# FFN heads: low parts of seven weight chunks formed by an adding DMA, and the last tile's norm and stores rearranged

## The chip, the core and the metric

The kernel runs on one core of a Trainium2 chip. The time is that of one execution on the device, in microseconds (us). The core's engines run side by side, each its own list of instructions: TensorE (PE, matrix products; PEld is its loading of weights), VectorE (DVE), ScalarE (ACT), GpSimd (POOL) and SyncE (SP, which here issues DMA transfers). They wait for each other through semaphores.

## The reference

Two layers on 512 tokens of width 1024, all in float32. Each layer has a mixer (layer 0: dilated attention beside a state-space model; layer 1: a recurrent block) and a SwiGLU feed-forward network (FFN) with 2816 hidden columns. Only the FFN and the norms around it matter here:

```
def rms_norm(x, g):
    y = x32 * lax.rsqrt(jnp.mean(x32 * x32, axis=-1, keepdims=True) + NORM_EPS) * g

def swiglu(x, w_gate, w_up, w_down):
    return (jax.nn.silu(x @ w_gate) * (x @ w_up)) @ w_down

for layer in range(DEPTH):
    ...
    hn = rms_norm(x, norm_ffn_pre[layer])
    ff = swiglu(hn, ffn_w_gate[layer], ffn_w_up[layer], ffn_w_down[layer])
    x = x + rms_norm(ff, norm_ffn_post[layer])
```

## The kernel before, in words

**Products in parts.** Every float32 operand of a matmul is split into a high part, rounded to the format `fp32r` that PE reads, and a low part, the raw value minus the high part. A product is then three matmuls: high by high, high by low, low by high. For weights the class `Chunk` does it, in half-chunks of 128x512 (four row blocks of 128 weights by 128 columns, 256 KB): the raw half is loaded by SP (L216), ACT copies it to the high part (L240), DVE subtracts the high part from the raw one (L241). Tiles are named after it: `wraw_`, `whi_`, `wlo_`, then the chunk.

**The FFN's entry** (`ffn_up`, called for layer 0 as `f0` and for layer 1 as `f1`). The weights of gate and up are taken as 44 column chunks of 128, gate and up in turn. The first four chunks (NFIRST) are multiplied half by half while the mixer's norm is still finishing the second half of the tokens; their banks carry the names `mo0b` and `mo1b`. Then come two "plain" chunks, `p4` (gate) and `p5` (up), 24 matmuls of 128x512 each into banks `f0b` (`f1b` in layer 1). Between these PE puts the norm's row, `bc_f`: four small matmuls that spread the reciprocal root `rsy_f` over the partitions. That root is made by DVE (`rst_f`, L380) from PE's sums `ns_mo` and raised to -1/2 by POOL (L383).

**The pairs.** The other 38 chunks are taken as pairs, one gate and one up chunk (n = 3 to 21), in a form of Strassen's scheme: seven products of half size instead of eight. `pair_weights` forms sums of the quarters of both chunks on DVE (L664 to L667) and makes four chunks of them: `a` (the gate chunk itself, but for a half that is used before and changed after), `c`, `d` (up) and `b`. On the side of the tokens ACT scales the inputs (`xa_f`, `xb_f`, L686 and L687), DVE forms the sums (L691 to L694), and ACT and DVE split them (`th_f`, `tl_f`). Products go to banks `f00b` to `f03b`. After the first products of a pair ACT copies out `pu_f` (L738) and `pv_f` (L742); only then may PE add the next products to the same banks ("onto").

**The end** (`ffn_last`). The down projection of layer 1 leaves each tile of 128 tokens in two banks of 512 columns. Per half, ACT sums squares (L850), POOL scales them (L852 for the first half, L854 and L855 for the second) and takes the power -1/2 (L856), DVE multiplies by the norm's weights (L858) and then by the root, adding the residual (L861); SP stores each half (256 KB).

**What sets the order.** The framework's scheduler orders each engine's list by its own estimates, except for stretches that the kernel pins to program order; the FFN's entry is not pinned. Weight tiles live in a pool of places that are handed on in the order in which they are given back; a load waits until the place's last reader is done. POOL has 58 instructions in the whole program and issues the small vector loads at the start on its own DMA queue; all weights come through SP's.

Of the kernel before, what the change touches and what calls it, by code (L numbers as in the profile page):

```python
# [19 lines left out]
P = 128  # L20
S = 512
# [73 lines left out]
def hybrid_trunk(  # L95
# [125 lines left out]
    class Chunk:  # L221


        def __init__(self, raw, nm, alloc=None, view=None, base=None, eng=None):
# [3 lines left out]
            for i, src in enumerate(raw.parts):  # L228
# [10 lines left out]
                if view is None:  # L239
                    act.activation(hi, src, AF.Copy)  # L240
                    eng.tensor_tensor(lo, src, hi.bitcast(F32), op=ALU.subtract)  # L241
# [376 lines left out]
    def ffn_up(layer, xh, xl, first, nsum, nm, hp):  # L618
# [37 lines left out]
        def pair_weights(n, alloc=None, base=None):  # L656

            r0, r1 = [Raw(NF, P, f"{nm}{n}{i}", cols2[2 * n + i][0][:, n * P:(n + 1) * P].rearrange(
                "(k p) n -> p k n", p=P), base=base) for i in range(2)]
            (a11, a12), (a21, a22) = r0.parts, r1.parts  # L660
            rs = Raw(NF, P, f"s_{nm}{n}", base=base)
# [11 lines left out]
        plain = [Chunk(Raw(NF, P, f"{nm}p{i}", cols2[i][0][:, cols2[i][1]:cols2[i][1] + P].rearrange(
            "(k p) n -> p k n", p=P), base=sb), f"{nm}p{i}",
            alloc=lambda name: hp.tile([P, S], F32R, tag=f"hh{next(own)}", name=name))
            for i in range(NFIRST, 2 * NPLAIN)]
# [26 lines left out]
        wa, wc, wd, wb = pair_weights(NPLAIN)  # L703
# [99 lines left out]
    def ffn_last(xh, xl, first, nsum):  # L803
# [37 lines left out]
        for t in range(NT):  # L841
# [4 lines left out]
            for h in range(2):  # L846
# [4 lines left out]
                if h == 0:  # L851
                    pool.tensor_scalar(s0, ss[:, 0:1], 1.0 / D, eps[:, t:t + 1], op0=ALU.mult, op1=ALU.add)  # L852
                else:
                    pool.tensor_scalar(r, ss[:, 1:2], 1.0 / D, None, op0=ALU.mult)  # L854
                    pool.tensor_tensor(r, r, s0, op=ALU.add)  # L855
# [4 lines left out]
            for h, y in enumerate(ys):  # L860
                dve.scalar_tensor_tensor(y, y, r, xk[2 * t + h], op0=ALU.mult, op1=ALU.add)  # L861
                nc.sync.dma_start(out[0, t * P:(t + 1) * P, h * 512:(h + 1) * 512], y)
# [838 lines left out]
```

## Time and profile before

| | |
|---|---|
| median of three timed runs | 1160.72 us (1160.39 to 1165.26) |
| profiled execution | 1165.47 us, span of its trace 1163.7 us |
| PE busy | 1117.9 us, 96% of the span |
| DVE busy | 887.0 us, 76% |
| ACT busy | 624.7 us, 54% |
| POOL busy | 25.1 us, 2% |
| 256 KB weight load on SP's queue, issue to landing | 2.7 to 4.8 us, median by tensor |

A row of the trace reads: start in us, duration in us, engine, line and operation, output<-inputs, partitions x elements, and in square brackets how long the engine had been idle ahead of it and which instruction ended that wait. "x4" after a row stands for four in a run of the same form. Matmuls overlap: the next one starts before the end of the one before is noted, so their rate is read from starts. An engine of 96% can still stand still at single places, and it is by stages that one sees where.

### The profile page before, as it was taken

The numbers are of one execution on the slowest core, as the hardware profiler recorded it, in microseconds if no ns is written. First come the engines' busy times: TensorE is split into PE (matmuls) and PEld (weight loads), VectorE is DVE, ScalarE is ACT, GpSimd is POOL, SyncE is SP. The second block draws the span as 40 slices with busy tenths as digits, with TensorE's granted clock in tenths as the row PEclk, the third lists the DMA queues.
The fourth block names the chain that finished last, engine by engine and source line by source line (L and its number), as shares of the span: only waits on it lengthen the run. The fifth ranks groups of instructions, "written<-read, shape, count | busy, mean of one in ns | idle before, by whom it ended". The sixth has DMA issues, their size and how long they took to land.

```text
span 1163.7 us, 19752 instructions
## 1 busy us (share of the span) xinstructions
PE 1117.9 (96%) x7310; PEld 992.1 (85%) x7310; DVE 887.0 (76%) x1899; ACT 624.7 (54%) x1280; POOL 25.1 (2%) x58
## 2 busy tenths in 40 slices
PE   6999899999899999999999999899999999999997
PEld 6877666889899999988889887689899999988886
DVE  7989675479999989882348877858999989884224
ACT  7556577357755554652344479644855455582221
POOL 1000010000000000000000000000000000000001
PEclk9999989999999999999999999899999999999999
DMA  8534410531433332433330432250243323324211
GB/s 212 144 118 134 107 47 1 162 92 28 125 105 94 96 101 83 122 98 97 118 100 10 118 96 85 65 171 19 79 122 94 107 76 107 119 92 127 91 64 72
DMA packets 165560, 113.42 MB, mean 97 GB/s; under 512 B 26852, under 2 KB 142296, under 8 KB 165464
## 3 DMA queue, kind: packets, MB, share of 16 engines
q1 hardware_dynamic: 162168, 109.95, 32.3%
q10 hardware_dynamic: 3040, 2.17, 0.7%
q8 instruction: 57, 0.93, 0.3%
q14 instruction: 39, 0.32, 0.1%
q0 software_dynamic: 256, 0.06, 0.0%
HBM read 103.75 MB, written 4.19 MB: 93 GB/s over the span
## 4 chain that ended last, share of the span: by engine, by line
PE 76%; ACT 8%; DVE 7%; DMA 6%; issue 2%; SPq 0%; ACTq 0%; DVEq 0%; POOLq 0%; POOL 0%
PE fo L170 10%; PE op_fd L170 10%; PE op_mo L170 7%; PE f12b L170 4%; PE f10b L170 4%; PE f02b L170 4%; PE f11b L170 4%; PE f00b L170 4%; PE f01b L170 4%; PE qkv L170 3%; DMA wraw_f<-in_ffn_w_gate_dram 2%; PE f03b L170 2%; PE f13b L170 2%; PE xbb L170 2%; PE ub L170 1%
## 5 line engine op out<-in xcount | busy, mean ns | idle before, releaser
L241 DVE TENSOR_TENSOR wlo_fo<-wraw_fo,whi_fo 128x512 fp32r<-128x512 f32 x44 | 30.2, 691 | 63.5 <-PE fo L170 60.6
L170 PE MATMUL op_fd<-hi_f,wlo_fd 128*128 128x512 f32 (+1 forms) x200 | 73.5, 367 | 0.0
L170 PE MATMUL op_fd<-lo_f,whi_fd 128*128 128x512 f32 (+1 forms) x200 | 73.4, 367 | 0.0
L170 PE MATMUL op_fd<-hi_f,whi_fd 128*128 128x512 f32 (+1 forms) x200 | 72.5, 369 | 0.0
L170 PE MATMUL fo<-wlo_fo,hi_f 128*128 128x512 f32 x176 | 69.5, 395 | 0.0
L170 PE MATMUL fo<-whi_fo,hi_f 128*128 128x512 f32 x176 | 69.3, 397 | 0.2 <-ACT whi_fo L240 0.2
L241 DVE TENSOR_TENSOR wlo_fd<-wraw_fd,whi_fd 128x512 fp32r<-128x512 f32 x44 | 30.1, 690 | 51.5 <-ACT whi_fd L240 45.1
L170 PE MATMUL fo<-whi_fo,lo_f 128*128 128x512 f32 x176 | 69.3, 394 | 0.0
L240 ACT ACTIVATE whi_fo<-wraw_fo 128x512 fp32r<-128x512 f32 x44 | 27.4, 631 | 71.7 <-DMA wraw_fo<-in_ffn_w_down_dram 46.6
L240 ACT ACTIVATE whi_fd<-wraw_fd 128x512 fp32r<-128x512 f32 x44 | 27.6, 628 | 60.4 <-DMA wraw_fd<-in_ffn_w_down_dram 36.5
L170 PEld LDWEIGHTS op_fd<-hi_f,whi_fd 128*128 128x128 f32 x200 | 37.6, 188 | 6.9 <-ACT hi_f L769 0.2
L170 PEld LDWEIGHTS op_fd<-hi_f,wlo_fd 128*128 128x128 f32 x200 | 37.6, 188 | 6.7
L170 PEld LDWEIGHTS op_fd<-lo_f,whi_fd 128*128 128x128 f32 x200 | 37.6, 188 | 6.7
L170 PE MATMUL qkv<-whi_qkv,xh_m 128*128 128x512 f32 x96 | 40.5, 427 | 0.0
L170 PEld LDWEIGHTS fo<-whi_fo,hi_f 128*128 128x128 f32 x176 | 33.1, 188 | 8.3 <-ACT whi_fo L240 0.6
L170 PEld LDWEIGHTS fo<-whi_fo,lo_f 128*128 128x128 f32 x176 | 33.1, 188 | 7.9
L170 PEld LDWEIGHTS fo<-wlo_fo,hi_f 128*128 128x128 f32 x176 | 33.0, 188 | 7.5
L170 PE MATMUL qkv<-wlo_qkv,xh_m 128*128 128x512 f32 x96 | 38.4, 400 | 0.0
L170 PE MATMUL qkv<-whi_qkv,xl_m 128*128 128x512 f32 x96 | 38.1, 397 | 0.0
L241 DVE TENSOR_TENSOR wlo_mo<-wraw_mo,whi_mo 128x512 fp32r<-128x512 f32 x32 | 21.4, 688 | 21.4 <-ACT whi_mo L240 21.4
L664 DVE TENSOR_TENSOR wraw_s_f<-wraw_f,wraw_f 128x512 f32<-128x512 f32 x38 | 26.0, 685 | 13.2 <-DMA wraw_f<-in_ffn_w_up_dram 11.3
L170 PE MATMUL op_mo<-y1l,whi_mo 128*128 128x256 f32 (+1 forms) x88 | 30.8, 349 | 4.1 <-DVE y1l L1628 4.1
(1922 smaller groups left out, 4197.2 us busy)
## 6 DMA issues: line engine op xcount, KB each, us to landing
wraw_f<-in_ffn_w_gate_dram SPq DMA_DIRECT2D x84, 256.0 KB, 3.1
wraw_f<-in_ffn_w_up_dram SPq DMA_DIRECT2D x84, 256.0 KB, 3.3
wraw_fd<-in_ffn_w_down_dram SPq DMA_DIRECT2D x44, 256.0 KB, 2.7
wraw_fo<-in_ffn_w_down_dram SPq DMA_DIRECT2D x44, 256.0 KB, 2.9
wraw_qkv<-in_ev_w_in_dram SPq DMA_DIRECT2D x24, 256.0 KB, 3.6
wraw_mo<-in_ev_w_out_dram SPq DMA_DIRECT2D x16, 256.0 KB, 4.8
wraw_xb<-in_od_w_in_dram SPq DMA_DIRECT2D x16, 256.0 KB, 2.8
wraw_gg<-in_od_w_in_dram SPq DMA_DIRECT2D x16, 256.0 KB, 3.0
```

The source lines that it names most:

```text
L170: self.pin(nc.tensor.matmul(o, lhsT=lhsT, rhs=rhs, start=start, stop=stop, **kw))
L240: act.activation(hi, src, AF.Copy)
L241: eng.tensor_tensor(lo, src, hi.bitcast(F32), op=ALU.subtract)
L664: dve.tensor_tensor(s1, a21, a22, op=ALU.add)
```

## The change: what it does

Seven half-chunks in each layer's FFN get their low part another way: both halves of `p4` and of `p5`, both halves of chunk `a` and the second half of chunk `d` of the first pair (n = 3). DVE's subtraction is gone. Instead ACT writes the negated raw half, rounded to `fp32r`, into the low part's tile, and POOL issues a DMA that loads the same half of the weights from memory once more and adds it to what lies there, so that raw minus high remains. These are the half-chunks whose raw values stand in memory as they are; the other chunks of the pair are sums made on the chip.

At the end, the two scalings of the sum of squares move from POOL to DVE, for every tile, and become two instructions instead of three; the power stays on POOL. For the last tile the final add and the store go in halves of 256 columns: four adds and four stores of 128 KB, and the second store of each pair is issued by ACT instead of SP.

```diff
@@ class Chunk
-        def __init__(self, raw, nm, alloc=None, view=None, base=None, eng=None):
+        def __init__(self, raw, nm, alloc=None, view=None, base=None, eng=None, dram=None):
...
                     act.activation(hi, src, AF.Copy)
-                    eng.tensor_tensor(lo, src, hi.bitcast(F32), op=ALU.subtract)
+                    if dram is not None and dram[i] is not None:
+
+                        act.activation(lo, src, AF.Copy, scale=-1.0)
+                        pool.dma_start(lo, dram[i], accum_op=ALU.add)
+                    else:
+                        eng.tensor_tensor(lo, src, hi.bitcast(F32), op=ALU.subtract)
...
+        def src_of(i):
+            w, c0 = cols2[i]
+            return w[:, c0:c0 + P].rearrange("(k p) n -> p k n", p=P)
+
+        def pair_weights(n, by_load=False):
...
-            return [Chunk(t, f"{nm}{n}{q}", alloc=alloc) for t, q in ((r0, "a"), (rs, "c"), (r1, "d"), (rt, "b"))]
+            same = {}
+            if by_load:
+                u, v = src_of(2 * n), src_of(2 * n + 1)
+                same = {"a": [u[:, 0:HK], u[:, HK:NF]], "d": [None, v[:, HK:NF]]}
+            return [Chunk(t, f"{nm}{n}{q}", dram=same.get(q))
+                    for t, q in ((r0, "a"), (rs, "c"), (r1, "d"), (rt, "b"))]
...
+        plain = [Chunk(Raw(NF, P, f"{nm}p{i}", src_of(i), base=sb), f"{nm}p{i}",
+                       alloc=lambda name: hp.tile([P, S], F32R, tag=f"hh{next(own)}", name=name),
+                       dram=[src_of(i)[:, 0:HK], src_of(i)[:, HK:NF]])
+                 for i in range(NFIRST, 2 * NPLAIN)]
...
-        wa, wc, wd, wb = pair_weights(NPLAIN)
+        wa, wc, wd, wb = pair_weights(NPLAIN, True)
@@ ffn_last
                 if h == 0:
-                    pool.tensor_scalar(s0, ss[:, 0:1], 1.0 / D, eps[:, t:t + 1], op0=ALU.mult, op1=ALU.add)
+                    dve.scalar_tensor_tensor(s0, ss[:, 0:1], 1.0 / D, eps[:, t:t + 1], op0=ALU.mult, op1=ALU.add)
                 else:
-                    pool.tensor_scalar(r, ss[:, 1:2], 1.0 / D, None, op0=ALU.mult)
-                    pool.tensor_tensor(r, r, s0, op=ALU.add)
+                    dve.scalar_tensor_tensor(r, ss[:, 1:2], 1.0 / D, s0, op0=ALU.mult, op1=ALU.add)
                     pool.tensor_tensor(r, r, neghalf[:, 0:1], op=ALU.pow)
...
             for h, y in enumerate(ys):
-                dve.scalar_tensor_tensor(y, y, r, xk[2 * t + h], op0=ALU.mult, op1=ALU.add)
-                nc.sync.dma_start(out[0, t * P:(t + 1) * P, h * 512:(h + 1) * 512], y)
+                for q in (HS if t == NT - 1 else [slice(0, S)]):
+                    dve.scalar_tensor_tensor(y[:, q], y[:, q], r, xk[2 * t + h][:, q], op0=ALU.mult, op1=ALU.add)
+                    c = h * 512 + q.start
+                    (nc.scalar if q.start else nc.sync).dma_start(
+                        out[0, t * P:(t + 1) * P, c:c + q.stop - q.start], y[:, q])
```

The scheduler rearranges the FFN's entry on all engines. Three places matter. In the rows below the numbers behind a name tell instances apart: `f0p4_0` is layer 0, chunk p4, first half. The layer 1 order is of the same kind.

On ACT, layer 0, from the first high part of a plain chunk on, before:

```order
L240 ACTIVATE whi_f0p4_0_3483<-wraw_f0p4_0_3479 128x512
L240 ACTIVATE whi_f0p4_1_3487<-wraw_f0p4_4_3481 128x512
L240 ACTIVATE whi_f0p5_0_3495<-wraw_f0p5_0_3491 128x512
L240 ACTIVATE whi_f0p5_1_3499<-wraw_f0p5_4_3493 128x512
L686 ACTIVATE xa_f00_3505<-xT_0_147,cols_143 128x512
L687 ACTIVATE xb_f00_3506<-xT_4_151,cols_143 128x512
```

and with the change:

```order
L240 ACTIVATE whi_f0p4_0_3483<-wraw_f0p4_0_3479 128x512
L243 ACTIVATE wlo_f0p4_0_3484<-wraw_f0p4_0_3479 128x512
L240 ACTIVATE whi_f0p4_1_3488<-wraw_f0p4_4_3481 128x512
L243 ACTIVATE wlo_f0p4_1_3489<-wraw_f0p4_4_3481 128x512
L240 ACTIVATE whi_f0p5_0_3497<-wraw_f0p5_0_3493 128x512
L243 ACTIVATE wlo_f0p5_0_3498<-wraw_f0p5_0_3493 128x512
L240 ACTIVATE whi_f0p5_1_3502<-wraw_f0p5_4_3495 128x512
L243 ACTIVATE wlo_f0p5_1_3503<-wraw_f0p5_4_3495 128x512
L699 ACTIVATE xa_f00_3509<-xT_0_147,cols_143 128x512
```

Four negations (L243) have come in between; `xa_f` (L686, now L699) stands four places later.

On PE, layer 0, the start of the plain chunks, before:

```order
L170 MATMUL f0b5_3654<-xh_mo00_2988,whi_f0p5_0_3495 128x512
L170 MATMUL f0b5_3654<-xl_mo00_2996,whi_f0p5_0_3495 128x512
L170 MATMUL f0b5_3654<-xh_mo00_2988,wlo_f0p5_0_3496 128x512
L170 MATMUL f0b5_3654<-xh_mo01_2989,whi_f0p5_0_3495 128x512
L170 MATMUL f0b5_3654<-xl_mo01_2997,whi_f0p5_0_3495 128x512
L170 MATMUL f0b5_3654<-xh_mo01_2989,wlo_f0p5_0_3496 128x512
```

and with the change:

```order
L170 MATMUL f0b4_3633<-xh_mo00_2988,whi_f0p4_0_3483 128x512
L170 MATMUL f0b4_3633<-xl_mo00_2996,whi_f0p4_0_3483 128x512
L170 MATMUL f0b5_3661<-xh_mo00_2988,whi_f0p5_0_3497 128x512
L170 MATMUL f0b5_3661<-xl_mo00_2996,whi_f0p5_0_3497 128x512
L170 MATMUL bc_f0_3472<-cst_63,rsy_f0_3468 128x128 x4
L170 MATMUL f0b4_3633<-xh_mo00_2988,wlo_f0p4_0_3484 128x512
L170 MATMUL f0b4_3633<-xh_mo01_2989,whi_f0p4_0_3483 128x512
```

Before, PE began with p5 and had its low part in third place; the `bc_f` group came after 25 matmuls. Now both chunks begin with their two products on the high part, the four `bc_f` come next, and the first product with a low part, that of p4's first half, is behind them.

On POOL, between the mixer's last root and the FFN's, with the change (before, `rsy_f0` followed `rsy_mo01` at once, and `rsy_fd00` came next):

```order
L388 TENSOR_TENSOR rsy_mo01_3222<-rst_mo01_3221,neghalf_133 128x2
L244 DMA wlo_f03a_1_3594<-in_ffn_w_gate_dram 128x4x128
L244 DMA wlo_f0p4_0_3484<-in_ffn_w_gate_dram 128x4x128
L388 TENSOR_TENSOR rsy_f0_3468<-rst_f0_3467,neghalf_133 128x4
L244 DMA wlo_f0p4_1_3489<-in_ffn_w_gate_dram 128x4x128
L244 DMA wlo_f0p5_0_3498<-in_ffn_w_up_dram 128x4x128
L244 DMA wlo_f0p5_1_3503<-in_ffn_w_up_dram 128x4x128
L244 DMA wlo_f03d_1_3611<-in_ffn_w_up_dram 128x4x128
L244 DMA wlo_f03a_0_3589<-in_ffn_w_gate_dram 128x4x128
L388 TENSOR_TENSOR rsy_fd00_7491<-rst_fd00_7490,neghalf_133 128x2
```

Two adding DMAs (L244) stand ahead of the root `rsy_f0` and five behind it, in the order in which POOL issues them. In layer 1 the order is the same.

More of the change, by code (lines that the diff above doesn't have):

```diff
@@ L654, in ffn_up @@
         mid()
-        def pair_weights(n, alloc=None, base=None):
-            r0, r1 = [Raw(NF, P, f"{nm}{n}{i}", cols2[2 * n + i][0][:, n * P:(n + 1) * P].rearrange(
-                "(k p) n -> p k n", p=P), base=base) for i in range(2)]
+        def src_of(i):
+            w, c0 = cols2[i]
+            return w[:, c0:c0 + P].rearrange("(k p) n -> p k n", p=P)
+        def pair_weights(n, by_load=False):
+            r0, r1 = [Raw(NF, P, f"{nm}{n}{i}", src_of(2 * n + i)) for i in range(2)]
             (a11, a12), (a21, a22) = r0.parts, r1.parts
-            rs = Raw(NF, P, f"s_{nm}{n}", base=base)
+            rs = Raw(NF, P, f"s_{nm}{n}")
             rt = Raw(HK, P, f"t_{nm}{n}")
@@ L672, in ffn_up @@
             retired.add((hp, f"hh{q}"))
[L673 to L676, printed above, removed]
+        plain = [Chunk(Raw(NF, P, f"{nm}p{i}", src_of(i), base=sb), f"{nm}p{i}",
+                       alloc=lambda name: hp.tile([P, S], F32R, tag=f"hh{next(own)}", name=name),
+                       dram=[src_of(i)[:, 0:HK], src_of(i)[:, HK:NF]])
+                 for i in range(NFIRST, 2 * NPLAIN)]
         t1 = [(xh[k][:, HS[1]], xl[k][:, HS[1]]) for k in range(HK)]
```

## The prediction, made before the changed kernel ran

> **What bounds the kernel now.** I read the page first: shares per engine and the chain of waits.
>
> ```profile
> PE 1117.9 (96%) x7310; PEld 992.1 (85%) x7310; DVE 887.0 (76%) x1899; ACT 624.7 (54%) x1280; POOL 25.1 (2%) x58
> PE 76%; ACT 8%; DVE 7%; DMA 6%; issue 2%; SPq 0%; ACTq 0%; DVEq 0%; POOLq 0%; POOL 0%
> ```
>
> TensorE is busy for 96% of the span. So taking work from VectorE (DVE) pays only where TensorE stands still, and everything turns on where that is. The window table, cut at the stages of the FFN entry, tells it (columns: stretch, length, busy time of PE, PEld, DVE, ACT, POOL, clock, DMA share, GB/s).
>
> ```profile
> 284.36:296.45 12.09, 12.09 (x59) 9.91 (x57) 11.93 (x27) 12.00 (x25) 1.01 (x1) 1.00 0.32 87
> 296.45:312.00 15.55, 12.34 (x92) 11.11 (x90) 15.55 (x34) 10.68 (x22) 0.00 (x0) 1.00 0.35 100
> 324.00:344.00 20.00, 20.00 (x170) 20.00 (x170) 19.69 (x39) 8.54 (x17) 0.00 (x0) 1.00 0.33 94
> 818.50:831.10 12.60, 12.60 (x61) 10.25 (x60) 12.60 (x27) 11.73 (x25) 1.25 (x1) 1.00 0.29 84
> 831.10:852.00 20.90, 17.68 (x136) 16.32 (x135) 20.90 (x44) 15.84 (x31) 0.00 (x0) 1.00 0.45 129
> ```
>
> While the plain chunks are multiplied (rows one and four), PE is full, and DVE and ACT are both full behind it. In the first pair (rows two and five) PE lacks 15.55 - 12.34 = 3.2 us in layer 0 and 20.90 - 17.68 = 3.2 us in layer 1, with DVE full throughout. From 324 on PE is full again: 170 matmuls of 128x256 in 20.00 us, 0.12 us each. So 6.4 us can be had at the heads, if all of it goes. What ends PE's waits there:
>
> ```profile
> 300.11 0.39 PE L170 MATMUL f00b<-xh_mo,whi_f03a 128*128 128x256 f32 x1 [0.65 <-ACT pu_f L738]
> ...
> 311.99 0.39 PE L170 MATMUL f00b<-xh_mo,whi_f05a 128*128 128x256 f32 x1 [1.57 <-ACT whi_f05a L240]
> ...
> 835.38 0.38 PE L170 MATMUL f10b<-xh_mo,whi_f13a 128*128 128x256 f32 x1 [1.46 <-ACT pu_f L738]
> 839.08 0.38 PE L170 MATMUL f12b<-xh_mo,whi_f13c 128*128 128x256 f32 x1 [0.24 <-ACT pv_f L742]
> ...
> 848.18 0.38 PE L170 MATMUL f10b<-xh_mo,wlo_f15a 128*128 128x256 f32 x1 [0.90 <-DVE wlo_f15a L241]
> 851.52 0.39 PE L170 MATMUL f11b<-th_f,whi_f15b 128*128 128x256 f32 x1 [0.44 <-DVE pu_f L753]
> ```
>
> The first wait of each layer, and the largest of layer 0, end with **ACT**, not DVE. The change takes work from DVE and puts as much on ACT, ahead of exactly these instructions. That is the core of the forecast.
>
> **The change part by part.** *Heads, DVE.* Seven subtractions of 128x512 per layer go.
>
> ```profile
> 282.42 1.88 DVE L241 TENSOR_TENSOR wlo_f0p<-wraw_f0p,whi_f0p 128x512 fp32r<-128x512 f32 x3
> ...
> 818.03 0.16 DVE L380 TENSOR_SCALAR rst_f<-ns_mo 128x4 f32<-128x4 f32 x1 [0.37 <-PE ns_mo L170]
> ```
>
> Three in 1.88 us, the last some 0.68 long, so 0.60 us each and 4.2 us a layer. Those that stand ahead of `rst_f` (three in layer 0, two in layer 1) free nothing that counts: `rst_f` waits for PE's sums of the norm anyway. Some 2.4 us of lead for DVE remain in layer 0, less what DVE then waits for ACT's high parts; I take 1 to 2.4 us.
>
> *Heads, ACT.* Seven negations of 128x512 come; six of them stand between the first head and `pu_f`.
>
> ```profile
> 281.55 2.18 ACT L240 ACTIVATE whi_f0p<-wraw_f0p 128x512 fp32r<-128x512 f32 x4
> ...
> 299.70 0.36 ACT L738 ACTIVATE pu_f<-f00b 128x256 f32<-128x256 f32 x1
> ...
> 311.31 0.63 ACT L240 ACTIVATE whi_f05a<-wraw_f 128x512 fp32r<-128x512 f32 x1 [2.69 <-DMA wraw_f<-in_ffn_w_gate_dram]
> ...
> 815.51 2.18 ACT L240 ACTIVATE whi_f1p<-wraw_f1p 128x512 fp32r<-128x512 f32 x4
> ...
> 825.19 0.63 ACT L240 ACTIVATE whi_f15a<-wraw_f 128x512 fp32r<-128x512 f32 x1 [0.87 <-DMA wraw_f<-in_ffn_w_gate_dram]
> ...
> 834.96 0.36 ACT L738 ACTIVATE pu_f<-f10b 128x256 f32<-128x256 f32 x1
> ```
>
> Four high parts take 2.18 us, one alone 0.63: (2.18 - 0.63)/3 = 0.52 us each. Six negations are 3.1 us on an engine that was 12.00 of 12.09 us busy. The new order also puts one 128x512 (0.52) more ahead of `pu_f` in layer 0, and one 128x512 and one 128x256 (about 0.3) behind it. Layer 0: 3.1 + 0.5 - 0.5 - 0.3 = 2.8, so `pu_f` moves from 299.70 to 302.5 and PE goes on 0.4 later, at 302.9 where it was 300.11. Layer 1: no such extra one, and the 0.87 us idle above is filled: 3.1 - 0.8 - 0.9 = 1.4, so PE goes on at 836.8 where it was 835.38.
>
> *The adding DMA.* No row of this program shows one. The nearest rows:
>
> ```profile
> vec<-in_norm_mix_pre_dram SPq DMA_DIRECT2D x1, 8.0 KB, 1.9
> ...
> vec<-in_norm_mix_post_dram POOLq DMA_DIRECT2D x1, 8.0 KB, 3.3
> ...
> wraw_f0p<-in_ffn_w_gate_dram SPq DMA_DIRECT2D x2, 256.0 KB, 3.1
> ...
> xtok<-in_x_dram SPq DMA_DIRECT2D x6, 256.0 KB, 6.8
> ```
>
> The lower bound is the plain 256 KB load, 3.1 us from issue to landing. POOL's queue costs 3.3 - 1.9 = 1.4 more for equal bytes. The bytes themselves are 3.1 - 1.9 = 1.2, and an adding transfer has to read the source and the tile it adds to, so 2.4. My estimate is 1.9 + 1.4 + 2.4 = 5.7 us. Upper bound: the slow load's bytes (6.8 - 1.9 = 4.9) doubled, plus 3.3: 13.1 us. I take 5.7, since the load of the very same weights shows 3.1, and the 6.8 belongs to a crowded start.
>
> The Trainium skill (Collectives: The Full Stack, "The bandwidth ceiling: the fold count and why AG ≠ RS ≠ AR") says that a reducing transfer is slower because its add takes two source reads, which halved the rate it measured; that speaks against the change as my doubling does. Its fit for this path (DMA: Bandwidth & Descriptors, "Anatomy of one DMA — SWDGE (gpsimd) path"), 2.0 us plus bytes at 436 GB/s, would give 2.6 us plain as an estimate; the row of 3.3 us for 8 KB is already above that. By either page the sum below stays as it is.
>
> Who waits for the first one:
>
> ```profile
> 284.36 0.40 PE L170 MATMUL f0b<-xh_mo,whi_f0p 128*128 128x512 f32 x1
> 284.60 0.39 PE L170 MATMUL f0b<-xl_mo,whi_f0p 128*128 128x512 f32 x1
> ...
> 290.19 1.05 PE L170 MATMUL bc_f<-cst,rsy_f 128*128 128x128 f32 x8
> 291.00 0.48 PE L170 MATMUL f0b<-xh_mo,wlo_f0p 128*128 128x512 f32 x1
> ```
>
> ```profile
> 284.46 1.01 POOL L383 TENSOR_TENSOR rsy_f<-rst_f,neghalf 128x4 f32<-128x4 f32 x1 [19.64 <-DVE rst_f L380]
> 818.27 1.47 POOL L383 TENSOR_TENSOR rsy_f<-rst_f,neghalf 128x4 f32<-128x4 f32 x1 [16.94 <-DVE rst_f L380]
> ```
>
> PE now has four products before the first low part, and `bc_f` among them. Layer 0: four at 0.24 from 284.36 is 285.3; `rsy_f` is there at 285.47; `bc_f` takes 291.00 - 290.19 = 0.8, so PE asks for the low part at 286.3. Its negation is ACT's second instruction after 281.55, done at 282.7, and lands at 282.7 + 5.7 = 288.4. **PE waits 2.1 us where it was full.** The plain chunks end at 296.45 + 2.1 + 0.2 = 298.7, and 27 products of 0.12 later PE stands at 301.9 before the wait for `pu_f`, which ends at 302.9 anyway. So this wait is hidden by the other, up to a landing of 5.7 + 1.0 = 6.7 us. Layer 1, by the same steps: PE asks at 818.27 + 1.47 + 0.8 = 820.5, the negation is done at 816.7, the landing at 822.4, a wait of 1.9; the plain chunks end at 833.2, 27 products later it is 836.4, so it is hidden up to 5.7 + 0.4 = 6.1 us. Every microsecond beyond costs one, in each layer. The later adding transfers are needed several microseconds after the first, p5's after all 24 products of p4 (5.6 us). POOL's issue work, seven times the row
>
> ```profile
> 2.49 0.49 POOL L303 DMA_DIRECT2D vec<-in_norm_ffn_post_dram  x1
> ```
>
> or up to twice that, falls on an engine that has only `rsy_f` here; two issues ahead of `rsy_f` end before `rst_f` does. At zero, then, unless an issue waits in POOL's order for a late negation.
>
> *What is late next.* Layer 0: the wait for `whi_f05a` (1.57) came from a load issued only when DVE's last x-sum freed its place:
>
> ```profile
> 306.59 0.37 SPq L216 DMA_DIRECT2D wraw_f<-in_ffn_w_gate_dram  x1
> ```
>
> That is 4.7 us before 311.31. DVE gets there earlier now. Position 91 of the pair, at 311.99 before, lies about 64 products (7.7 us) after the restart at 302.9: 310.6 with no further wait, about 312.5 if `pv_f` is held behind that same `whi_f05a` in ACT's new order. Middle 311.5: **-0.5 us** (-1.4 to +0.5). Layer 1: +1.4 at the restart, and the waits of 0.24, 0.90 and 0.44 behind it are swallowed by the shift and by DVE's lead: **-0.2 us** (-0.9 to +1.4).
>
> *Tail.*
>
> ```profile
> 1157.51 0.19 ACT L850 ACTIVATION_READ_ACCUMULATOR fsq<-fo 128x1 f32 x1
> ```
>
> ```profile
> 1157.79 0.22 POOL L854 TENSOR_SCALAR rsy_fin<-ss 128x1 f32<-128x1 f32 x1 [2.50 <-ACT fsq L850]
> ...
> 1158.37 0.57 POOL L856 TENSOR_TENSOR rsy_fin<-rsy_fin,neghalf 128x1 f32<-128x1 f32 x1
> ```
>
> ```profile
> 1158.97 1.41 DVE L861 SCALAR_TENSOR_TENSOR yo<-yo,rsy_fin,xT 128x512 f32<-128x512 f32 x2 [0.54 <-POOL rsy_fin L856]
> ```
>
> ```profile
> 1160.40:1160.90 0.50, 0.00 (x0) 0.00 (x0) 0.00 (x0) 0.00 (x0) 0.00 (x0) 1.00 0.61 229
> ...
> 1161.90:1162.40 0.50, 0.00 (x0) 0.00 (x0) 0.00 (x0) 0.00 (x0) 0.00 (x0) 0.65 0.13 45
> ```
>
> Two POOL steps (1157.79 to 1158.37) become one small DVE instruction, as short as `rst_f` (0.16): the power starts at 1157.9 and ends at 1158.5. DVE then has the last product with the norm's weights still to finish, so the adds start at 1158.6, 0.4 earlier. Four halves at about 0.43 (half of 0.70, and some fixed part) end at 1160.3, hardly earlier than 1160.38, but the last store now carries 128 KB, not 256: with data running from 1160.6 to 1161.97 for 512 KB, a quarter is 0.34 where a half was 0.69. **-0.5 us** (-0.9 to +0.3, if an issue on ACT is slower than one on SP).
>
> Sum: -0.5 - 0.2 - 0.5 = **-1.2 us**. Against the profiled execution's own 1165.47 us that is 1164.3; that execution lies 0.4% above the median of the timed runs, 1160.72, so on their scale I predict **1159.5 us**.
>
> **The rivals.** *DVE's relief pays in full.* For it: DVE is full in both first-pair windows. Against: PE's waits there end with ACT. If ACT's order did not matter, the 6.4 us go and the tail's 0.5: 1160.7 - 6.9 = 1153.8; with half of it 1157.
>
> *The adding DMA lands late, slower.* Place: PE's sixth instruction of the plain chunks, waiting for `wlo_f0p4_0`, with all 48 products queued behind it. It decides from 6.1 to 6.7 us on. At 10 us it costs 3.3 + 3.9 - 1.2 = +6.0: 1166.7. At 13.1 us 6.4 + 7.0 - 1.2: 1173. For it: seven transfers of 256 KB on a queue that moved 0.06 MB in all before, and `rsy_f` at 1.47 us in layer 1 against 1.01, so POOL is not undisturbed beside a full DVE. Against: the sum of 5.7. The Trainium skill (SBUF — State Buffer, "Who interferes with whom") says that DVE instructions with two SBUF inputs contend with a POOL instruction that reads SBUF, not with one that only writes; by it `rsy_f` is slowed and the making of descriptors is not, and the two rows of `rsy_f` agree as far as they go.
>
> *The reshuffled order.* The scheduler rearranges all three engines through the pairs, though PE is full there before. A wait like the 0.90 at 848.18 once more in each layer costs 1.8: 1161.3.
>
> **How the numbers follow.** Forecast 0.60, relief in full 0.16, late landing 0.16, reshuffle 0.08. The range 1154.5 to 1166.5 holds the forecast with its bounds (1157.5 to 1162.9: the terms' ends, -3.2 to +2.2, rarely together), half of the relief, and landings up to about 10 us; the ends of both rivals are left out. What a measurement here can tell from no change is 0.5%, 5.8 us: under 1154.9 is faster, over 1166.5 slower. Faster 0.13 (most of the full relief), slower 0.13 (landings beyond 10 us), same 0.74.
>
> **What would show it.** In the profile after: a PE wait of about 2 us at `f0b<-xh_mo,wlo_f0p` released by a DMA; `pu_f` on ACT some 2.8 and 1.4 us later against the start of the plain chunks; PE idle in the two first-pair windows no larger in sum with that wait than before; last DMA data about 0.5 us earlier after the last matmul. I am wrong if the landing is over 6.7 us, if the wait for `pu_f` does not move, or if PE stands still at a new place in later pairs.

## The result, and the profile after

The changed kernel takes **1176.42 us** (median of four runs, 1175.96 to 1177.45) beside 1162.15 us for the kernel before (four runs, 1160.39 to 1165.26): a ratio of 1.0119, 95% interval 1.0097 to 1.0141. The forecast was 1159.5 us, no measurable change. It is 14 us slower, beyond the range.

The page of the changed kernel (busy time per engine; shares of the chain of waits):

```profile
PE 1118.5 (95%) x7310; PEld 994.1 (85%) x7310; DVE 881.2 (75%) x1895; ACT 635.3 (54%) x1294; POOL 40.8 (3%) x60
PE 75%; DMA 8%; DVE 8%; ACT 7%; issue 2%; ACTq 0%; SPq 0%; POOLq 0%; DVEq 0%
```

PE does the same work in the same busy time (1117.9 before), while the span grows from 1163.7 to 1174.6: TensorE stands still longer, or runs at a lower clock. In the chain DMA grows from 6% to 8%. To see where, the span is cut at the first matmul of the stages:

| stretch, us | before | after |
|---|---|---|
| start to `f0b` (FFN of layer 0) | 284.4 | 281.9 |
| `f0b` to `fd0b` (gate and up, layer 0) | 334.5 | 340.8 |
| `fd0b` to `f1b` | 199.4 | 200.1 |
| `f1b` to the last `fo<-whi_fo,hi_f` | 337.8 | 344.6 |

The two FFN stretches lose 6.3 and 6.8 us. The profiled execution of before reached the first FFN 2.5 us later than the changed kernel's did. It was that much behind at the mixer's first root already (`rsy_mo` on POOL, 253.48 and 250.94), ahead of all that was changed; that is most of why the two spans differ by less than the medians. Within the stretch the loss comes at once: from `f0b` to the first product of the first pair (`f00b`) it was 297.04 - 284.36 = 12.7 us, and is 300.33 - 281.9 = 18.4 now, 5.7 more.

That stage in the window table, before and then after (the changed kernel is 2.5 us further on at the same time; stretch, length, busy time of PE, PEld, DVE, ACT, POOL, clock, DMA share, GB/s):

```profile
284.00:296.00 12.00, 12.00 (x59) 9.91 (x59) 11.84 (x28) 11.91 (x25) 1.01 (x1) 1.00 0.29 78
```

```profile
284.00:296.00 12.00, 10.29 (x47) 8.23 (x46) 4.41 (x11) 11.62 (x23) 5.85 (x5) 1.00 1.24 189
...
296.00:298.00 2.00, 0.87 (x5) 0.46 (x3) 0.00 (x0) 0.28 (x1) 0.00 (x0) 1.00 0.39 112
298.00:300.00 2.00, 0.00 (x0) 0.00 (x0) 1.62 (x3) 0.90 (x2) 0.00 (x0) 0.71 0.00 0
300.00:302.00 2.00, 1.67 (x8) 1.68 (x9) 2.00 (x5) 1.97 (x4) 0.00 (x0) 0.50 0.00 0
302.00:304.00 2.00, 2.00 (x11) 2.00 (x11) 2.00 (x6) 1.98 (x5) 0.00 (x0) 0.50 0.14 38
304.00:306.00 2.00, 1.89 (x10) 1.59 (x10) 2.00 (x7) 0.60 (x2) 0.00 (x0) 0.58 0.76 224
```

DVE was full and is busy for 4.41 of 12 us: far more idle than the seven subtractions (4.2 us) that went. The DMA engines' share went from 0.29 to 1.24, that is, they are full. Then PE stands still, and goes on at half clock. DVE's own rows say what it stood for (timeline of the changed kernel, idle time and its releaser in brackets):

```profile
289.36 0.69 DVE L246 TENSOR_TENSOR wlo_f03c<-wraw_s_f,whi_f03c 128x512 fp32r<-128x512 f32 x1 [2.21 <-ACT whi_f03c L240]
289.97 0.68 DVE L246 TENSOR_TENSOR wlo_f03b<-wraw_t_f,whi_f03b 128x512 fp32r<-128x512 f32 x1
298.38 0.69 DVE L672 TENSOR_TENSOR wraw_s_f<-wraw_f,wraw_f 128x512 f32<-128x512 f32 x1 [7.73 <-DMA wraw_f<-in_ffn_w_up_dram]
...
299.59 1.28 DVE L652 TENSOR_TENSOR gt_f<-mo0b,bcs_f 128x512 f32<-128x512 f32 x2
...
840.11 0.69 DVE L672 TENSOR_TENSOR wraw_s_f<-wraw_f,wraw_f 128x512 f32<-128x512 f32 x1 [7.56 <-DMA wraw_f<-in_ffn_w_up_dram]
```

The long wait is in front of L672, the first sum of **pair 5's** weights. PE reads the first chunk of pair 5 only from 314.7 us on, and those made from this sum (`b`, `c`) from 326.6 on. Behind it in DVE's order stand the two `gt_f`, which empty the bank that pair 3 is to be multiplied into. In the kernel before, the same instruction (L664, whose sum ACT reads for `whi_f05c` at 299.96) stood behind the `gt_f` and waited for nothing:

```profile
296.47 0.69 DVE L647 TENSOR_TENSOR gt_f<-mo0b,bcs_f 128x512 f32<-128x512 f32 x1
...
299.21 0.69 DVE L664 TENSOR_TENSOR wraw_s_f<-wraw_f,wraw_f 128x512 f32<-128x512 f32 x1
```

So DVE stood 2.21 + 7.73 = 9.9 us where 4.2 us had been saved: 5.7 us net, as much as that stage lost. PE's waits follow (timeline of the changed kernel):

```profile
286.23 0.50 PE L170 MATMUL f0b<-xh_mo,wlo_f0p 128*128 128x512 f32 x1 [1.71 <-DMA wlo_f0p<-in_ffn_w_gate_dram]
300.33 0.58 PE L170 MATMUL f00b<-xh_mo,whi_f03a 128*128 128x256 f32 x1 [3.45 <-DVE gt_f L652]
323.67 0.39 PE L170 MATMUL f00b<-xh_mo,whi_f04a 128*128 128x256 f32 x1 [1.92 <-ACT pu_f L751]
...
827.10 0.50 PE L170 MATMUL f1b<-xh_mo,wlo_f1p 128*128 128x512 f32 x1 [0.94 <-DMA wlo_f1p<-in_ffn_w_gate_dram]
841.54 0.54 PE L170 MATMUL f10b<-xh_mo,whi_f13a 128*128 128x256 f32 x1 [3.66 <-DVE gt_f L652]
865.93 0.58 PE L170 MATMUL f10b<-xh_mo,whi_f14a 128*128 128x256 f32 x1 [2.88 <-ACT pu_f L751]
```

Why the load was not there is told by the chain of waits (start, duration, what), from the first adding DMA to ACT's part of pair 5:

```profile
280.76 5.42 DMA wlo_f0p<-in_ffn_w_gate_dram
...
286.23 5.20 PE f0b L170 x22
291.43 6.83 DMA wraw_f<-in_ffn_w_up_dram
...
298.38 0.70 DVE wraw_s_f L672
...
299.10 0.63 ACT whi_f05c L240
```

The load begins when PE has done 22 further products of the plain chunks (26 in all), which frees its place: 291.43 - 281.9 = 9.5 us after `f0b` starts. DVE's being early can't hasten it, and the late adding DMA holds it up. It then takes 6.83 us, where loads of this tensor take 3.2 (median of 84), because it shares the DMA engines with the adding transfers (with a quarter of their bytes, in a run below, the loads of this tensor take 3.0 there). The adding DMAs of that stretch, behind the dots all loads of this tensor, and the queues of the whole program (share of 16 engines' span):

```profile
wlo_f0p<-in_ffn_w_gate_dram POOLq DMA_DIRECT2D x2, 256.0 KB, 5.3
wlo_f0p<-in_ffn_w_up_dram POOLq DMA_DIRECT2D x2, 256.0 KB, 6.3
...
wlo_f03d<-in_ffn_w_up_dram POOLq DMA_DIRECT2D x1, 256.0 KB, 7.7
...
wraw_f<-in_ffn_w_up_dram SPq DMA_DIRECT2D x84, 256.0 KB, 3.2
```

```profile
q1 hardware_dynamic: 162168, 109.68, 31.8%
q0 software_dynamic: 7648, 3.73, 2.6%
```

Per MB the adding queue holds the engines for 2.6/3.73 = 0.70% of the span, the plain one for 31.8/109.68 = 0.29%: 2.4 times as long. The packets are not of one size on average, but from 276 to 300 us they are: 3696 packets, 1.84 MB, which hold the engines for 62.5% of that stretch as adding transfers, and for 27.3% as the plain loads of the kernel before.

The second wait, 1.92 and 2.88 us for `pu_f`, has the same form on ACT: a later pair's instruction that waits for its load, with `pu_f` behind it (timeline of the changed kernel):

```profile
299.10 0.63 ACT L240 ACTIVATE whi_f05c<-wraw_s_f 128x512 fp32r<-128x512 f32 x1 [2.82 <-DVE wraw_s_f L672]
...
322.19 0.63 ACT L240 ACTIVATE whi_f07a<-wraw_f 128x512 fp32r<-128x512 f32 x1 [2.93 <-DMA wraw_f<-in_ffn_w_gate_dram]
...
323.25 0.36 ACT L751 ACTIVATE pu_f<-f00b 128x256 f32<-128x256 f32 x1
...
863.94 0.63 ACT L240 ACTIVATE whi_f17a<-wraw_f 128x512 fp32r<-128x512 f32 x1 [4.15 <-DMA wraw_f<-in_ffn_w_gate_dram]
```

The kernel before has this place too, but small: ACT stands 1.80 us, and PE behind it 0.45 us for the same `pu_f` (at 321.11).

```profile
319.63 0.63 ACT L240 ACTIVATE whi_f07a<-wraw_f 128x512 fp32r<-128x512 f32 x1 [1.80 <-DMA wraw_f<-in_ffn_w_gate_dram]
```

### The profile page after: what moved, and what is told of

It is laid out like the page before. It is cut to its first block, busy times and chain, and to the rows that moved or that the text cites. A ratio compares the mean times of both kernels' runs of the same rounds, so it can differ in the third digit from the quotient of the medians.

```text
span 1174.6 us, 19798 instructions
## 1 busy us (share of the span) xinstructions
PE 1118.5 (95%) x7310; PEld 994.1 (85%) x7310; DVE 881.2 (75%) x1895; ACT 635.3 (54%) x1294; POOL 40.8 (3%) x60
## 3 DMA queue, kind: packets, MB, share of 16 engines
q1 hardware_dynamic: 162168, 109.68, 31.8%
q0 software_dynamic: 7648, 3.73, 2.6%
## 4 chain that ended last, share of the span: by engine, by line
PE 75%; DMA 8%; DVE 8%; ACT 7%; issue 2%; ACTq 0%; SPq 0%; POOLq 0%; DVEq 0%
PE fo L170 10%; PE op_fd L170 10%; PE op_mo L170 7%; PE f01b L170 4%; PE f11b L170 4%; PE f12b L170 4%; PE f10b L170 4%; PE f02b L170 4%; PE f00b L170 4%; PE qkv L170 3%; PE f13b L170 2%; PE f03b L170 2%; PE xbb L170 2%; DMA wraw_f<-in_ffn_w_up_dram 1%; PE ub L170 1%
## 5 line engine op out<-in xcount | busy, mean ns | idle before, releaser
L672 DVE TENSOR_TENSOR wraw_s_f<-wraw_f,wraw_f 128x512 f32<-128x512 f32 x38 | 26.0, 684 | 26.1 <-DMA wraw_f<-in_ffn_w_up_dram 23.3
```

The source lines that it names most:

```text
L672: dve.tensor_tensor(s1, a21, a22, op=ALU.add)
```

## The experiments

The theory that this profile suggests: **the order**. With less work estimated for DVE, the scheduler let DVE run ahead into pair 5, and engines that work off their lists in order stand at loads that are not there. The rivals: **the load itself** (the adding transfers take the DMA engines, and without that the new order would do no harm); **ACT's negations**, as forecast; and that **DVE's relief** is worth nothing here. All ratios are against runs of the kernel before on the same chip in the same series (medians 1163.73, 1162.98 and 1163.12 us).

### The end alone

Before, with only the change of `ffn_last`:

```diff
-                    pool.tensor_scalar(r, ss[:, 1:2], 1.0 / D, None, op0=ALU.mult)
-                    pool.tensor_tensor(r, r, s0, op=ALU.add)
+                    dve.scalar_tensor_tensor(r, ss[:, 1:2], 1.0 / D, s0, op0=ALU.mult, op1=ALU.add)
...
+                for q in (HS if t == NT - 1 else [slice(0, S)]):
+                    dve.scalar_tensor_tensor(y[:, q], y[:, q], r, xk[2 * t + h][:, q], op0=ALU.mult, op1=ALU.add)
```

> The heads as before, only the change at the end (two VectorE steps instead of three POOL steps, quarters of the last tile, two stores issued by ACT). Theory: none of the loss belongs to it; from the last matmul to the span's end 7.2 us become about 6.7, the time 0.5 us lower than before (-0.9 to +0.3). Rival: the stores through ACT cost, then the time is over 1162.

1163.11 us, ratio 1.0004 (0.9981 to 1.0026). From the start of the last `fsq` to the end of the span it is 6.27 us, where the kernel before has 1163.7 - 1157.02 = 6.68: 0.4 us gained, too little for the timed runs to show. The end has no part in the loss.

### DVE's order

The whole change, but pair 5's first sum may not be issued ahead of the second low part of the pair's x-sums on DVE:

```diff
-            dve.tensor_tensor(s1, a21, a22, op=ALU.add)
+            with ExitStack() as order:
+                if n == NPLAIN + 2:
+                    order.enter_context(tc.issue_after(env["tli", 1]))
+                dve.tensor_tensor(s1, a21, a22, op=ALU.add)
```

> The whole change, with one instruction held back on VectorE: the first sum of pair 5 (L672 of the changed kernel) may go only behind the second tl_f of the second x-sum. Theory A (the loss is VectorE standing at this sum for 7.7 us, waiting for a weight load, with the head's gt_f and all x-sums behind it): that wait falls below 1 us in both layers, PE's waits of 3.5 and 3.7 us for gt_f go, the time is 1162 to 1166. Rival B (the adding transfers slow every load, so PE stands still wherever the sum is put): 1171 or more.

1168.18 us, ratio 1.0038 (1.0020 to 1.0056): by the ratios 0.81 of the 1.19%, some 9 of the 14 us, are back with all seven adding DMAs in place. The time lies between the two expectations. DVE's 7.73 us wait is gone. What is left is the wait of the second kind (ACT's row, then PE's, in this run):

```profile
318.44 0.63 ACT L240 ACTIVATE whi_f06a<-wraw_f 128x512 fp32r<-128x512 f32 x1 [4.08 <-DMA wraw_f<-in_ffn_w_gate_dram]
```

```profile
321.23 0.39 PE L170 MATMUL f00b<-xh_mo,whi_f04a 128*128 128x256 f32 x1 [3.01 <-ACT pu_f L755]
```

ACT stands 4.08 us for pair 6's load, with `pu_f` of pair 4 behind it (at 320.80 now); PE then stands 3.01 us for `pu_f`.

### Adding DMAs for the plain chunks alone

```diff
-        wa, wc, wd, wb = pair_weights(NPLAIN, True)
+        wa, wc, wd, wb = pair_weights(NPLAIN)
```

> The change for the two plain chunks alone: four adding transfers in a layer, the first pair's low parts by VectorE as before; the end as changed. The scheduler puts pair 5's first sum behind gt_f here. Theory A (order and a late load): no wait for gt_f on PE, the time 1160 to 1165. Rival B (adding transfers cost by their number): four sevenths of 14, so about 1170.

1170.03 us, ratio 1.0064 (1.0035 to 1.0093). Four instead of seven already cost half of the loss. The time is the rival's (a cost by the number of transfers); the theory's 1160 to 1165 missed. As it said, PE has no wait for `gt_f`, but DVE still stands 4.45 and 3.27 us at pair 5's first sum, and `pu_f` is the largest of PE's waits in layer 1 (2.3 us). The run with four and both holds, below, decides between the two.

### A quarter of the adding DMA's bytes

The adding DMA loads and adds one of the four row blocks (in the other three the low part stays the negated raw weights):

```diff
-                        pool.dma_start(lo, dram[i], accum_op=ALU.add)
+                        pool.dma_start(lo[:, 0:1], dram[i][:, 0:1], accum_op=ALU.add)
```

> The whole change, but each adding DMA moves only a quarter of its bytes (one row block of 128 of four; the other three quarters of these low parts stay the negated raw weights, so the output is not the reference's). The order on VectorE has pair 5's first sum just as early, one place earlier still. If the load of pair 5 is late because the adding transfers fill the DMA engines (share 1.3 of them between 286 and 296 us): the load lands 3 to 4 us after issue instead of 6.8, VectorE's wait falls from 7.7 to about 4 us, PE's wait for gt_f goes, the time is 1162 to 1166. If the early place of the sum alone is the cause: the wait on PE stays over 2 us, the time 1170 or more.

1176.65 us, ratio 1.0106 (1.0069 to 1.0143): as slow as the whole change. The DMA theory's expectation missed. Its profile (of its fastest execution, 1168.09 us) shows that the edit did what it should, both to the transfers and to DVE's wait:

```profile
wlo_f0p<-in_ffn_w_gate_dram POOLq DMA_DIRECT2D x2, 64.0 KB, 3.1
```

```profile
289.58 0.69 DVE L672 TENSOR_TENSOR wraw_s_f<-wraw_f,wraw_f 128x512 f32<-128x512 f32 x1 [2.80 <-DMA wraw_f<-in_ffn_w_up_dram]
```

```profile
314.81 0.63 ACT L240 ACTIVATE whi_f07a<-wraw_f 128x512 fp32r<-128x512 f32 x1 [4.33 <-DMA wraw_f<-in_ffn_w_gate_dram]
```

DVE waits 2.80 instead of 7.73, but ACT stands 4.33 us at pair 7's load and PE then 2.4 and, in layer 1, 3.7 us for `pu_f`. In this execution the two FFN stretches are still 4.4 and 4.5 us longer than before. Contention makes the first wait long; taking it away hands the loss on to the next place of the same kind.

### Both holds

The hold on DVE, and one on ACT: the high part of chunk `a` of pairs 6 and 7 not ahead of pair 4's `pu_f`.

```diff
+            with ExitStack() as order:
+                if n in (NPLAIN + 3, NPLAIN + 4):
+                    order.enter_context(tc.issue_after(env["pui", NPLAIN + 1]))
+                first = Chunk(r0, f"{nm}{n}a", dram=same.get("a"))
```

> The whole change with two holds: pair 5's first sum on VectorE as in the run with the one hold, and besides on ScalarE the high parts of chunk a of pairs 6 and 7 only behind pu_f of pair 4. With the one hold ScalarE stood 4.1 and 3.8 us at these high parts, waiting for their loads, and PE 3.0 and 2.8 us for the pu_f behind them, with the granted clock at 0.50 for some 3.5 us after each. Theory (in-order engines held by a later pair's load): both PE waits fall below 1.5 us, the clock stays at 1.00 in the FFN entries, time 4 to 7 us below the one hold's, 1161 to 1165. Rival (those loads are needed then anyway, the wait only moves): within 2 us of the one hold's 1168.

1161.58 us, ratio 1.0002 (0.9976 to 1.0027). The loss is gone, with the change's whole work unchanged: seven negations, seven adding DMAs, seven subtractions fewer. So the loss hangs on the order. In the trace DVE's long wait is gone, PE waits 0.60 us for `pu_f` in layer 0, and the two FFN stretches are 333.6 and 338.3 us (334.5 and 337.8 before). One long wait has come, for the low part of chunk `a` in layer 1, and the clock is at 0.50 behind it (waits of PE in the whole program: total, times, longest; then a window):

```profile
PE f10b L170 <- DMA wlo_f13a<-in_ffn_w_gate_dram: 2.4, 1, 2.4
```

```profile
834.00:835.00 1.00, 1.00 (x7) 1.00 (x6) 1.00 (x4) 1.00 (x4) 0.00 (x0) 0.50 0.88 246
```

The kernel before was not run with the holds, so a small gain of their own is not excluded; of the waits that they are aimed at, its trace has only PE's 0.45 us.

### The hold on ACT alone

The same edit without the hold on DVE.

> The whole change with the hold on ScalarE alone (chunk a of pairs 6 and 7 behind pu_f of pair 4); pair 5's sum stays early on VectorE. If the two places add up: the 7.7 us wait on VectorE and PE's 3.5 us for gt_f stay, PE's later wait for pu_f goes, time 1168 to 1172. If the wait on VectorE alone carries the loss: 1174 or more. If the wait on ScalarE alone carries it: under 1165.

1173.13 us, ratio 1.0075 (1.0046 to 1.0104). The four corners are then 1.0119 (no hold), 1.0038 (DVE), 1.0075 (ACT), 1.0002 (both). The holds bring 0.81% and 0.44% alone and 1.17% together: within the intervals they add up, so DVE's and ACT's waits are two separate losses. With the ACT hold alone DVE stands 7.1 and 7.7 us at pair 5's sum, PE's wait for `gt_f` in layer 1 is that of the changed kernel (3.7 us), and no wait for `pu_f` is left. In layer 0 the wait for `gt_f` is only 0.73, since PE came late itself: it had stood 2.30 us for the first adding DMA and run at half clock behind it.

### POOL subtracts instead

No negation and no adding DMA; POOL does the seven subtractions:

```diff
-                        act.activation(lo, src, AF.Copy, scale=-1.0)
-                        pool.dma_start(lo, dram[i], accum_op=ALU.add)
+                        pool.tensor_tensor(lo, src, hi.bitcast(F32), op=ALU.subtract)
```

> The change without negations and adding DMAs: POOL itself subtracts, raw minus high, for the same seven half-chunks of a layer (a 128x512 operation of two inputs took POOL 1.04 us before). VectorE is relieved by the same 4.2 us a layer, ScalarE and the DMA engines carry nothing more. If the relief of VectorE pays as soon as nothing else is loaded: faster than before by 3 to 6 us, 1157 to 1161. If the relief reorders the entry so that engines stand at late loads whatever makes the low parts: slower than before by 2 to 10 us.

1174.35 us, ratio 1.0095 (1.0057 to 1.0132). ACT is free of the negations and no DMA is added, and it is as slow. But here another cost comes in (a row of POOL's, then DVE's):

```profile
290.57 1.59 POOL L243 TENSOR_TENSOR wlo_f03a<-wraw_f,whi_f03a 128x512 fp32r<-128x512 f32 x1
```

```profile
290.59 0.41 DVE L704 TENSOR_TENSOR wraw_tr_f<-xb_f,xa_f 128x256 f32<-128x256 f32 x1
290.93 1.79 DVE L674 TENSOR_TENSOR wraw_s_f<-wraw_f,wraw_t_f 128x512 f32<-128x512 f32 x1
292.64 1.52 DVE L705 TENSOR_TENSOR wraw_tr_f<-xb_f,wraw_tz_f 128x256 f32<-128x256 f32 x1
```

While POOL subtracts, DVE's 128x256 sums take up to 1.52 instead of 0.41 us (the one that starts together with POOL's does not), and a 128x512 one 1.79 instead of 0.68. So this run does not tell the rivals apart: its loss has a cause of its own. The Trainium skill (SBUF — State Buffer, "Who interferes with whom") says that a DVE instruction with two SBUF inputs contends with a GpSimd instruction that reads SBUF; the rows of 1.79 and 1.52 agree, the 0.41 at 290.59 does not show it.

### The work left out

The seven low parts are not formed at all (the high part stands in for them):

```diff
-                        act.activation(lo, src, AF.Copy, scale=-1.0)
-                        pool.dma_start(lo, dram[i], accum_op=ALU.add)
+                        self.parts[-1] = [hi, hi]
```

> The seven low parts of a layer are not formed at all: PE takes the high part in place of the low one (so the output is not the reference's). No subtraction, negation or adding DMA; all else as changed. This is the most the relief can bring in the order that the scheduler gives then. If the relief pays: 6 us or more below before, under 1158. If the order that follows the relief is the trouble: VectorE or ScalarE stand 2 us or more at a load, PE waits over 2 us with half the clock after, and the time is not below before by more than 2 us.

1161.01 us, ratio 0.9980 (0.9962 to 0.9998). This is the change at the price of nothing: no negation, no transfer. It gains some 2 us, not the 6.4 us in which PE lacked work. Its timeline shows the same pattern, smaller:

```profile
295.17 0.69 DVE L671 TENSOR_TENSOR wraw_s_f<-wraw_f,wraw_f 128x512 f32<-128x512 f32 x1 [1.94 <-DMA wraw_f<-in_ffn_w_up_dram]
```

DVE arrives early at pair 5's load and stands; PE then waits in later pairs, among them 2.5 us for `whi_f04b` and 1.5 for `whi_f04c`. So an early DVE alone need not make the kernel slower: the loss of the change takes the negations or the transfers besides, or the order that comes with them.

### More work for DVE

Before, with six additions of 128x512 more on DVE per layer, whose output nobody reads:

```diff
+            if n == NPLAIN:
+                with tc.issue_after(last):
+                    for _ in range(6):
+                        dve.tensor_tensor(dummy, xT[0], xT[1], op=ALU.add)
```

> The kernel before with more work for VectorE: in each FFN layer six additions of 128x512 into a tile that nobody reads, 0.60 us each, behind the last sum of the first pair. If VectorE bounds the entry (it is busy throughout it), each layer pays about 3.6 us, the time is 6 to 10 us above before, more where a PE wait brings the half clock. If ScalarE's order sets PE's waits there, as forecast: within 3 us of before.

1171.41 us, ratio 1.0069 (1.0045 to 1.0093): about 8 us for 12 x 0.60 = 7.2 us of work. The rival that DVE's work is worth nothing at the entry falls. The price is not simply DVE's time, though. In this trace PE's waits of 1.25 and 1.31 us in layer 0 are followed by half clock from 313.6 to 320.4 us, which the kernel before has nowhere in its FFN:

```profile
315.00:316.00 1.00, 1.00 (x7) 1.00 (x6) 1.00 (x3) 0.44 (x1) 0.00 (x0) 0.50 0.00 0
```

Summed over windows of 0.25 us (PE's busy time, times what the clock is short of 1.00), half clock costs 3.1 us in layer 0 and 1.7 in layer 1, more than half of the 8. Work added to DVE costs about 8 us here, and work taken away (8.4 us) brought back about 2 in the order that the scheduler then gave.

### Fewer adding DMAs, with both holds

First the four of the plain chunks (both holds, and `pair_weights(NPLAIN)` as above), which also tells what the adding DMAs of chunks `a` and `d` are worth:

> The four adding transfers of the plain chunks alone, with both holds; without the holds this stood at 1.0064 of before. Theory (the loss is in-order engines held by later pairs' loads): time within 2 us of before or below, as with seven transfers. Rival (the holds helped only the order that seven transfers gave): 1167 or more.

**1157.35 us, ratio 0.9945 (0.9924 to 0.9967)**: faster than both kernels, by some 6 us against before. In each layer's entry PE has one long wait, in layer 1 2.1 us for `whi_f14d`, in layer 0 that for the first adding DMA (waits of PE between 284 and 326 us: total, times, longest):

```profile
PE f0b L170 <- DMA wlo_f0p<-in_ffn_w_gate_dram: 1.9, 1, 1.9
```

and where PE used to run dry as the first pair began, it is now full, with DVE full beside it (windows of this run):

```profile
296.00:298.00 2.00, 2.00 (x19) 2.00 (x18) 2.00 (x6) 2.00 (x7) 0.00 (x0) 1.00 0.00 0
```

Then five: the halves that PE asks for first, `p4`'s first and chunk `a`'s first, go back to DVE.

```diff
-                same = {"a": [u[:, 0:HK], u[:, HK:NF]], "d": [None, v[:, HK:NF]]}
+                same = {"a": [None, u[:, HK:NF]], "d": [None, v[:, HK:NF]]}
...
-                       dram=[src_of(i)[:, 0:HK], src_of(i)[:, HK:NF]])
+                       dram=[src_of(i)[:, 0:HK] if i > NFIRST else None, src_of(i)[:, HK:NF]])
```

> Both holds, and five adding transfers in a layer instead of seven: the first halves of p4 and of chunk a go back to VectorE's subtraction, since with both holds PE still waited 1.7 and 0.9 us for the first and 2.4 us (layer 1, half clock after it) for the second of these. Theory: those waits go, VectorE is still relieved by 3.0 us a layer, time 2 to 5 us below before. Rival (nothing in the entry is left to be had, the kernel is bound by PE's work there): within 2 us of before.

1158.49 us, ratio 0.9959 (0.9940 to 0.9978). The same gain within the intervals as with four. That the gain is the change's and not the holds' own is likely by the waits that before has (0.45 us where the holds act), but no run shows it.

### A quarter of the bytes, with both holds

> Both holds, and adding DMAs that move a quarter of their bytes (three quarters of these low parts stay the negated raw weights, the output is not the reference's). Against the run with both holds and whole transfers it shows what the load on the DMA engines costs once the order is held. Contention theory: 2 us or more below that run's 1161.6 since loads land in 3 us and PE's waits for low parts shrink. Order theory: within 2 us of it; the quarter without holds cost 1176, so most of 15 us goes by order alone.

1156.69 us, ratio 0.9958 (0.9935 to 0.9981), beside 1.0002 for the whole bytes with the same holds. By the middle values the transfers' own time costs 0.4%, 5 us, but the intervals overlap, so this is not shown. Without the holds the same quarter gained nothing: what the transfers cost can only come out once the order is held.

## Why the prediction was wrong

**Right.** *The wait for the first adding DMA* came where it was put, at `f0b<-xh_mo,wlo_f0p`: 1.71 us in layer 0 (2.1 forecast) and 0.94 in layer 1 (1.9). The first product with a low part starts 4.4 and 4.3 us after the stage's first product, where the sum had 288.4 - 284.36 = 4.0 and 822.4 - 818.3 = 4.1. The waits came out shorter because `bc_f` came later: `rsy_f` took 1.49 and 1.92 us on POOL (1.01 and 1.47 before). The estimate of 5.7 us for the landing measured 5.4 from the issue in layer 0, 6.0 from the end of the negation; later ones took up to 8.7. *The tail* gained 0.4 us for 0.5 forecast: the adds start 1169.93 - 1168.82 = 1.11 us after the last square sum, where before they started 1158.97 - 1157.51 = 1.46 after it (the changed kernel's end):

```profile
1168.82 0.19 ACT L863 ACTIVATION_READ_ACCUMULATOR fsq<-fo 128x1 f32 x1
...
1169.93 1.67 DVE L874 SCALAR_TENSOR_TENSOR yo<-yo,rsy_fin,xT 128x256 f32<-128x256 f32 x4
```

**Wrong in size.** POOL's issue of an adding DMA takes 1.3 to 2.0 us of POOL (40.8 - 25.1 = 15.7 us more in all, net of the scalings that went), where 0.5 to 1.0 was said. In the changed kernel PE waits for no adding DMA after the first. With both holds it does (2.4 us for `wlo_f13a`); whether POOL's issues or the transfers made that one late was not told apart.

**Wrong in the core.** "The first wait of each layer, and the largest of layer 0, end with ACT, not DVE", and the forecast hung everything on ACT's 2.8 us more ahead of `pu_f`. After the change ACT was not late from work: it stood idle 2.82 us at 299.10, waiting for DVE's L672. `pu_f` of the first pair came 303.29 - 281.87 = 21.4 us after the stage's start (15.3 before; 2.8 more had been forecast), behind that same wait, and PE did not even wait for it: it stood for `gt_f`. In the kernel before ACT ended the small waits of the first pair, while DVE was busy for all 15.55 us of it and ACT for 10.68. By this, and since the run with more DVE work is slower, DVE and not ACT bound that stage; no run shows it by itself.

**The step that failed** is "What is late next", with the lead of "1 to 2.4 us" for DVE ahead of it. It counted DVE's relief as a lead that shortens waits (-0.5 and -0.2 us), kept DVE's list as it was, and did not ask which load DVE's next instructions need, nor who frees that load's place. Pair 5's load is issued 9.5 us after `f0b` starts, as before (9.7), because PE frees its place. DVE stood at pair 5's sum 290.65 - 281.87 = 8.8 us after `f0b`'s start, where it had come to it after 299.21 - 284.36 = 14.9; the load landed after 298.26 - 281.87 = 16.4. And the reordered list put the `gt_f`, on which PE's next bank hangs, behind this sum. The list of DVE is also the one that the part ahead of the prediction does not show. The measured term is +6.3 and +6.8 us where -0.5 and -0.2 stood.

**The rivals.** *The reshuffled order* named the right mechanism, an instruction placed ahead of a load in an order that the scheduler rearranged, and dismissed it since "PE is full there before"; it was priced at two waits of 0.90 us, with 0.08 of the chance. It measured 14 us: by the ratios DVE's hold alone recovers 9 and ACT's alone 5. *Late landing* had its place wrong: the first adding DMA was about on time, but the transfers together made another load slow. *Relief in full* falls by the run with the work left out, which gains 2 us and not 6.9. With the order held, though, the version with four adding DMAs gains 6 us, so the time was there to be had.

**What stays open.** How the 14 us divide between PE's waits and the half clock that follows them was not tried apart. By windows of 0.25 us half clock takes 2.6 us in layer 0 and 3.2 in layer 1 of the changed kernel, 5.8 of the 13.1 us that the two FFN stretches lose, and nothing in the FFN before. Which part of the added work makes the early order dear, the negations or the transfers, is not settled either: with a quarter of the bytes the kernel is as slow, with neither it is not slow, and POOL's run had a cost of its own. Why four adding DMAs gain and seven do not, with the same holds, was not isolated. The trace with seven has PE's waits of 0.66 and 2.37 us for chunk `a`'s low parts and 1.7 us of half clock behind the second, 4.7 in all, which the trace with four lacks; it has three negations more on ACT as well.

## What to carry to other kernels

When a scheduler orders the lists of engines that work in order, relief for one engine need not be a lead: here it pulled a later instruction forward until that stood at a load that can't be earlier, and everything behind it stood too. Before costing such a relief at a gain, look up for the next few instructions of the relieved engine which load each needs and what frees that load's place, and compare the new list of that engine, not only that of the engine that ends the waits. Where the order then does harm, it can be held by hand: three instructions held back in each layer brought back here all that the change had cost (1.2%).

## What the runs showed of the hardware

**The clock can halve after a stall of PE, and such a stall costs more than its length.** In the kernel before no window of the two FFN entries is under 1.00. In the changed kernel the clock falls to 0.50 after the waits of 3.45 and 3.66 us (the windows above; layer 1 below, with the wait of 2.88 ahead of the second row):

```profile
842.00:844.00 2.00, 2.00 (x11) 2.00 (x10) 2.00 (x5) 1.99 (x4) 0.00 (x0) 0.50 0.00 0
...
866.00:868.00 2.00, 2.00 (x9) 2.00 (x10) 2.00 (x6) 2.00 (x5) 0.00 (x0) 0.50 0.00 0
```

From 300 to 306 us PE was busy for 1.67 + 2.00 + 1.89 us at clocks of 0.50, 0.50 and 0.58: 1.67 x 0.50 + 2.00 x 0.50 + 1.89 x 0.42 = 2.6 us lost, on top of the wait of 3.45. The stretch at half clock lasts 3 to 7 us in the changed kernel, and from 838 to 849 us in the run with the hold on ACT alone. The length of a wait alone does not tell: 1.92 us for `pu_f` in the changed kernel left the clock at 1.00, and the same wait of 1.91 us in the run with four adding DMAs and no hold was followed by 0.53; 2.5 us (the work left out) left it, 2.4 (both holds, seven adding DMAs) did not. The shortest that were followed by 0.50 are one of 1.31 (more DVE work) and one of 0.94, 2 us behind one of 0.71 (hold on DVE, layer 1); the changed kernel's own 0.94, behind one of 0.70, was not. The Trainium skill (TensorE: Matmul & The Clock Gate, "Part 1: The HAM clock gate (the "warmup" mystery)") puts the fall after an idle window of about 3.4 us that runs freely. That equal waits end differently agrees with a window that does not start with the wait; that waits of 0.94 to 2.88 us were followed by half clock shows that staying under 3.4 us of idleness is no safe bound here.

**An adding DMA holds the DMA engines 2.4 times as long per byte as a plain load**, and seven of them in 12 us fill all 16 engines: the share stood at 1.24, and an unrelated load of 256 KB took 6.83 us instead of 3.2. Its issue on POOL did not slow DVE's two-input instructions (from 284.60 to 286.72 the 128x256 sums beside issues on POOL take 0.42 us each, the 128x512 one at 289.36 takes 0.69), while beside a subtraction on POOL most of them took two to four times as long.
